# Step tables read from the joined kernels, which are written block by block; small loads issued after a product

## The chip, the cores and the metric

One core of a Trainium2 chip. TensorE (PE; PEld is its weight load) multiplies, VectorE (DVE), ScalarE (ACT) and GpSimd (POOL) work element by element, SyncE (SP) and GpSimd issue DMAs. Each engine runs its own list of instructions in a fixed order. The metric is the device time of one execution in microseconds; the median of 3 runs is 1490.93 us (1490.72 to 1493.30).

## What is computed

Two blocks of two layers each on 256 tokens of 1024 features, all in float32. The first block: an even mixer, a banded attention, each followed by attention over a memory and by a squared-ReLU MLP. The second block, cut to what matters here:

```python
mix = diff_attention(u, w_qkv, q_gain, k_gain, lam_vecs, ...)   # layer 0: rotary tables times gains
h = h + mix; h = h + squared_relu_mlp_2(rms_norm(h), w_up, w_down)
mix = s5_layer(u, a_re, a_im, log_dt, b_re, b_im, c_re, c_im, d_skip, w_glu)   # layer 1
# per group of 16 features, 64 complex states, forward and backward:
states = associative_scan(a_bar, u @ b_bar);  y = (states @ c).real
y = y_forward + y_backward + d_skip * u;  val, gate = gelu(y) @ w_glu;  out = val * sigmoid(gate)
```

## The kernel before

Matrix products are made of three products of split operands: each weight is loaded into `raw`, ScalarE makes its rounded part `whi` (L47, L53), VectorE the rest `wlo` (L49, L58). `raw` has 4 buffers, `whi` and `wlo` 10 each; SyncE issues all weight loads in order, and waits there for a free buffer.

The state-space layer works in steps of 8 tokens. For each of 64 groups it needs tables that depend on parameters alone: `e` (tokens to states), `g` (states to tokens) and `t`, the step table, that takes 8 tokens directly to 8 tokens. They are made by `ssm_tables`, a generator over 16 blocks of 4 groups, and kept in DRAM. Blocks 0 to 7 are made during the last MLP of the first block (`first_block`, L1781), blocks 8 to 15 during the first MLP of the second (`second_block`, L1812). The MLP calls `step(1)` at 49 places (L392, L323, L367), which lets the generator go on by `rate` turns each; `step(1000)` at L397 drains it before the last products. The generator has 35 yields for eight blocks; the second one then runs `ssm_prefetch`, which loads the first tables of the state-space stage. The vector work of the tables is at lower priority (`self.low(90)`).

A block's lag kernels go from `kl` to `d_kl` in DRAM, a row of 144 for each of 4 x 2 x 16 (group, direction, feature). After the last of eight blocks two DMAs join the directions in `d_ks` (rows of 240, forward in 112:240, backward in 0:112; L1450, L1451). Eight DMAs (L1456) then write the table of 8 shifts, each a window of 128 at offset 16 r, to `d_tt`. All these are issued by GpSimd. `load_units` loads 8 groups of `d_tt` in one DMA of 512 KB from SyncE (L1482); there are 8 such units `t`. `load_phases` (L1494) loads the rotation tables `tbs` of the scan, also from SyncE.

`diff`, the attention between those two MLPs, issues six small loads at its start (L644 to L652), then `part(D)`, the products of the keys, then `rotations()` on VectorE (L657 to L674), which needs the loads. Ahead of it in program order stands the end of the MLP: `residual` for each half t of the tokens, with a root on GpSimd (L171), its product with `rsq` (L194), the addition to X (L200) and the transposes `tp` (L140) that the next products need.

The order on each engine is not the program's: a planner places each instruction by priority and by the time at which it reckons its inputs to be ready, and that order is then fixed.

Of the kernel before, what the change touches and what calls it, by code (L numbers as in the profile page):

```python
# [413 lines left out]
class Attn:  # L414
# [224 lines left out]
    def diff(self, pool, w_qkv, gain, q_gain, k_gain, lam_vecs, subln, w_o, cos2, sin2, done):  # L639

        nc = self.nc
        cs = pool.tile([128, 2, 64], F32, tag="cos", name="cos")
        sn = pool.tile([128, 2, 64], F32, tag="sin", name="sin")
        nc.sync.dma_start(out=cs, in_=cos2.rearrange("(t p) e -> p t e", p=128))  # L644
        nc.sync.dma_start(out=sn, in_=sin2.rearrange("(t p) e -> p t e", p=128))
        gq, gk = (pool.tile([128, 64], F32, tag="g" + nm, name="qkg") for nm in "qk")
        nc.sync.dma_start(out=gq, in_=q_gain.partition_broadcast(128))
        nc.sync.dma_start(out=gk, in_=k_gain.partition_broadcast(128))
        sg = pool.tile([128, KT], F32, tag="sg", name="sg")
        nc.sync.dma_start(out=sg, in_=subln)  # L650
        lv = pool.tile([128, 4, 64], F32, tag="lv", name="lv")
        nc.sync.dma_start(out=lv, in_=lam_vecs.partition_broadcast(128))  # L652
        nlam = pool.tile([128, 1], F32, tag="nlam", name="nlam")
        tabs = {}

        def rotations():
            for nm, g in (("k", gk), ("q", gq)):  # L657
                ta = pool.tile([128, 2, 64], F32, tag="ta" + nm, name="ta")
                tb = pool.tile([128, 2, 64], F32, tag="tb" + nm, name="tb")
                if nm == "q":  # L660
                    nc.vector.tensor_scalar(out=g, in0=g, scalar1=0.125, scalar2=None, op0=ALU.mult)
                for t in range(2):
                    nc.vector.tensor_tensor(out=ta[:, t, :], in0=cs[:, t, :], in1=g, op=ALU.mult)
                    nc.vector.tensor_tensor(out=tb[:, t, 0:32], in0=sn[:, t, 0:32], in1=g[:, 32:64], op=ALU.mult)
                    nc.vector.tensor_tensor(out=tb[:, t, 32:64], in0=sn[:, t, 32:64], in1=g[:, 0:32], op=ALU.mult)
                tabs[nm] = (ta, tb)
# [477 lines left out]
class Ssm:  # L1144
# [3 lines left out]
    def ssm_scratch(self, dram):  # L1148
# [6 lines left out]
        self.d_ks = dram.tile([NG, 16, 240], F32, name="d_ks")  # L1155
        self.d_tt = dram.tile([128, NG, 128], F32, name="d_tt")

# [212 lines left out]
    def ssm_tables(self, blocks, bc4, gain, d_rows, dmask):  # L1370
# [6 lines left out]
        with self.tc.tile_pool(name="tab", bufs=1, reuse_waits="tile") as pool:  # L1377
# [33 lines left out]
            def second(k, bc, bm, er, gr):  # L1411
                cr, ci = bc[:, :, 2], bc[:, :, 3]
                for g2 in range(2):
# [6 lines left out]
                    nc.gpsimd.dma_start(out=self.d_e[k, :, g2 * 512:g2 * 512 + 512], in_=eo.rearrange("p g r n -> p (g r n)"))  # L1420
                    yield
                ps = self.ps.tile([128, 144], F32, tag="ps", name="klag")
                for j in range(4):
# [10 lines left out]
                nc.gpsimd.dma_start(out=self.d_kl[k], in_=kl)  # L1434

            last = None
            for k in list(blocks) + [None]:
# [8 lines left out]
                yield  # L1446
            a0, a1 = blocks[0], blocks[-1] + 1
            kl5 = self.d_kl.rearrange("a (q d i) n -> a q d i n", q=4, d=2)
            ks = self.d_ks.rearrange("(a q) i n -> a q i n", q=4)
            nc.gpsimd.dma_start(out=ks[a0:a1, :, :, 112:240], in_=kl5[a0:a1, :, 0, :, 0:128])  # L1450
            nc.gpsimd.dma_start(out=ks[a0:a1, :, :, 0:112], in_=kl5[a0:a1, :, 1, :, 32:144])  # L1451
            yield
            n = 4 * (a1 - a0)
            for r in range(8):
                src = bass.AP(self.d_ks.tensor, self.d_ks.offset + 4 * a0 * 16 * 240 + r * 16, [[240, 16], [3840, n], [1, 128]])
                nc.gpsimd.dma_start(out=self.d_tt[r * 16:r * 16 + 16, 4 * a0:4 * a1, :], in_=src)  # L1456
            yield

    def ssm_prefetch(self):
# [9 lines left out]
        for q in range(4):  # L1469
            t = pool.tile([128, 1024], F32, name=f"e{q}")  # L1470
            self.load_units(t, "e", q)
        for q in range(2):
            self.load_units(pool.tile([128, 1024], F32, tag=f"w{q}", name=f"t{q}"), "t", q)

    def load_units(self, tile, kind, i, n=1):

        t = tile.rearrange("p (a n) -> p a n", n=1024)
        if kind == "t":
            src = self.d_tt[:, 8 * i:8 * (i + n), :].rearrange("p (a g) n -> p a (g n)", g=8)
        else:  # L1480
            src = (self.d_e if kind == "e" else self.d_g)[i:i + n].rearrange("a p n -> p a n")
        self.nc.sync.dma_start(out=t, in_=src)  # L1482
        for a in range(n):
# [7 lines left out]
    def load_phases(self, b):  # L1491

        t = self.pre.tile([128, 3, 16, 32], F32, tag="tbs", name="tbs", bufs=2)
        self.nc.sync.dma_start(out=t, in_=self.d_c[b].rearrange("p (a g c) -> p a g c", a=3, g=16))  # L1494
        self.tbs[b] = t
# [241 lines left out]
def first_block(c, A):  # L1737
    tc, nc = c.tc, c.nc
    for l in range(2):
# [38 lines left out]
        with tc.tile_pool(name=f"ff{l}", bufs=1, reuse_waits="tile") as pool:  # L1778
            if l == 1:
                c.later.append(lambda: reorder(c))  # L1780
            c.mlp(pool, A["w_ff1"][l], gc[2], A["w_ff2"][l], lambda t, a, q: c.residual(t, a, post, q), perm=l == 1,  # L1781
                  fill=tables(c, A, range(8)) if l == 1 else c.ssm_scalars(A["ssm_a_re_2"], A["ssm_a_im_2"], A["ssm_log_dt_2"], c.sgn),
                  rate=0.7 if l == 1 else 0.2)

# [14 lines left out]
def tables(c, A, blocks, last=False):  # L1799
    yield from c.ssm_tables(blocks, A["ssm_bc"], A["ssm_g"], c.d_rows, c.dmask)  # L1800
    if last:
        c.ssm_prefetch()


def second_block(c, A, out):
# [5 lines left out]
    with tc.tile_pool(name="ffb0", bufs=1, reuse_waits="tile") as pool:  # L1811
        c.mlp(pool, A["ffn_w_up_2"][0], c.gcols[:, 8, :], A["ffn_w_down_2"][0], lambda t, a, q: c.residual(t, a, None, q, feat=False),  # L1812
              fill=tables(c, A, range(8, 16), last=True), rate=0.85)
    with tc.tile_pool(name="ssm", bufs=1, reuse_waits="tile") as pool:
# [84 lines left out]
```

## Time and profile before

| | us |
|---|---|
| median of 3 runs | 1490.93 |
| profiled execution | 1488.93 |
| its span | 1487.2 |
| TensorE busy | 1414.7 |
| VectorE busy | 1103.8 |
| ScalarE busy | 859.4 |
| GpSimd busy (its DMA issues not counted) | 234.4 |

Times in rows are counted from the start of the span. A number after `[` is idle time of the engine before the instruction, and `<-` names what ended it. `SPq` is SyncE's DMA queue. Busy times of matrix products overlap, since they are pipelined.

### The profile page before, as it was taken

What the parts mean: (1) busy time and instruction counts of PE and PEld (TensorE: products, weight loads), DVE (VectorE), ACT (ScalarE), POOL (GpSimd) and SP (SyncE); (2) the same over time, 40 slices, a digit from 0 to 9 for tenths busy, and PEclk for the clock granted to TensorE, in tenths of its full rate; (3) what the DMA queues carried; (4) which work ended last, traced back from release to release, by engine and by line L of the source; (5) the groups of instructions that cost most, each with busy time, mean ns of one, the idle gap of its engine ahead of it and who ended that gap; (6) DMA issues with size and microseconds to landing.
All of it is one profiled execution on the core that took longest, in us unless ns stands there. A gap on an engine that the chain in (4) does not pass through costs nothing.

```text
span 1487.2 us, 25549 instructions
## 1 busy us (share of the span) xinstructions
PE 1414.7 (95%) x9668; PEld 1231.5 (83%) x9668; DVE 1103.8 (74%) x1965; ACT 859.4 (58%) x1480; POOL 234.4 (16%) x290
## 2 busy tenths in 40 slices
PE   8899999999999999999999789999999878999997
PEld 8897888998889798878888667888889666889895
DVE  7996658997676866569998589889995487665651
ACT  7475547565564665566656557667656463554540
POOL 1232001000010000014634210033551200000000
PEclk9999999999999999999999999999999998999999
DMA  8465535475875356366677734357779977455640
GB/s 302 143 198 170 185 125 177 157 257 193 287 256 184 119 180 200 112 207 207 220 242 265 254 124 142 100 161 241 238 236 334 346 280 262 153 187 180 210 159 29
DMA packets 121236, 298.26 MB, mean 201 GB/s; under 512 B 15129, under 2 KB 24121, under 8 KB 120473
## 3 DMA queue, kind: packets, MB, share of 16 engines
q1 hardware_dynamic: 113848, 271.40, 55.3%
q0 software_dynamic: 7264, 25.24, 4.6%
q8 instruction: 76, 1.25, 0.3%
q14 instruction: 48, 0.39, 0.1%
HBM read 270.15 MB, written 31.62 MB: 203 GB/s over the span
## 4 chain that ended last, share of the span: by engine, by line
PE 73%; DVE 13%; DMA 6%; issue 4%; ACT 3%; POOL 1%; SPq 0%; DVEq 0%; ACTq 0%; POOLq 0%
PE ffacc L217 7%; PE ffacc L219 7%; PE ffacc L218 7%; PE ffps L224 5%; PE ffps L226 5%; PE ffps L225 5%; PE pacc L219 4%; PE pacc L218 4%; PE pacc L217 4%; DVE wlo L58 3%; PE pb L225 3%; PE pb L224 3%; PE pb L226 3%; DMA raw<-in_w_ff 2%; PE ffps L219 2%
## 5 line engine op out<-in xcount | busy, mean ns | idle before, releaser
L58 DVE SCALAR_TENSOR_TENSOR wlo<-raw,gcols,whi 128x512 fp32r<-128x512 f32 (+1 forms) x456 | 356.7, 826 | 75.6 <-ACT whi L53 75.3
L53 ACT ACTIVATE whi<-raw,gcols 128x512 fp32r<-128x512 f32 (+1 forms) x456 | 317.0, 745 | 104.4 <-PE pb L226 17.3
L47 ACT ACTIVATE whi<-raw 128x1024 fp32r<-128x1024 f32 x176 | 182.8, 1055 | 155.6 <-DMA raw<-in_w_ff 59.3
L49 DVE TENSOR_TENSOR wlo<-raw,whi 128x1024 fp32r<-128x1024 f32 x172 | 210.1, 1241 | 84.1 <-ACT whi L47 80.1
L224 PE MATMUL ffps<-hh,whi 128*128 128x256 f32 x768 | 220.2, 287 | 2.7 <-ACT eo L1419 1.5
L226 PE MATMUL ffps<-hl,whi 128*128 128x256 f32 x768 | 218.2, 284 | 0.0
L225 PE MATMUL ffps<-hh,wlo 128*128 128x256 f32 x768 | 217.6, 283 | 0.0
L217 PE MATMUL ffacc<-whi,ah 128*128 128x512 f32 x512 | 204.7, 400 | 0.0
L219 PE MATMUL ffacc<-whi,al 128*128 128x512 f32 x512 | 202.2, 395 | 0.0
L218 PE MATMUL ffacc<-wlo,ah 128*128 128x512 f32 x512 | 202.1, 395 | 0.0
L224 PEld LDWEIGHTS ffps<-hh,whi 128*128 128x128 f32 x768 | 146.0, 190 | 5.3 <-ACT eo L1419 2.0
L225 PEld LDWEIGHTS ffps<-hh,wlo 128*128 128x128 f32 x768 | 145.7, 190 | 0.6
L226 PEld LDWEIGHTS ffps<-hl,whi 128*128 128x128 f32 x768 | 145.8, 190 | 0.0
L219 PEld LDWEIGHTS ffacc<-whi,al 128*128 128x128 f32 x512 | 96.4, 188 | 22.7
L217 PEld LDWEIGHTS ffacc<-whi,ah 128*128 128x128 f32 x512 | 96.5, 188 | 22.5 <-issue 1.8
L218 PEld LDWEIGHTS ffacc<-wlo,ah 128*128 128x128 f32 x512 | 96.5, 189 | 20.8
L225 PE MATMUL pb<-hh,wlo 128*128 128x256 f32 x352 | 101.2, 289 | 2.6 <-DVE wlo L58 2.6
L224 PE MATMUL pb<-hh,whi 128*128 128x256 f32 x352 | 101.2, 290 | 2.2 <-ACT whi L53 2.2
L226 PE MATMUL pb<-hl,whi 128*128 128x256 f32 x352 | 100.8, 287 | 0.0
L171 POOL TENSOR_TENSOR r<-r,mhalf 128x1 f32<-128x1 f32 x32 | 23.3, 730 | 463.9 <-DVE r L170 457.4
L303 ACT ACTIVATE relu<-ffps 128x512 f32<-128x512 f32 x64 | 43.8, 685 | 54.9 <-PE ffps L226 36.4
L225 PEld LDWEIGHTS pb<-hh,wlo 128*128 128x128 f32 x352 | 68.4, 195 | 3.4 <-DVE wlo L58 3.3
(488 smaller groups left out, 3024.9 us busy)
## 6 DMA issues: line engine op xcount, KB each, us to landing
raw<-in_w_ff SPq DMA_DIRECT2D x128, 512.0 KB, 4.6
raw<-in_ffn_w_up SPq DMA_DIRECT2D x64, 512.0 KB, 4.7
raw<-in_ffn_w_down SPq DMA_DIRECT2D x64, 512.0 KB, 4.6
raw<-in_w_mem_kv SPq DMA_DIRECT2D x32, 512.0 KB, 4.7
raw<-in_w_qkv SPq DMA_DIRECT2D x24, 512.0 KB, 4.7
raw<-in_attn_w_qkv SPq DMA_DIRECT2D x24, 512.0 KB, 5.0
raw<-in_w_in_ab SPq DMA_DIRECT2D x20, 512.0 KB, 6.5
raw<-in_w_mem_q SPq DMA_DIRECT2D x16, 512.0 KB, 4.6
```

Source lines behind the costliest of these rows:

```text
L47: nc.scalar.activation(out=hi, in_=src, func=AF.Copy)
L49: eng.tensor_tensor(out=lo, in0=src, in1=hi.bitcast(F32), op=ALU.subtract)
L53: nc.scalar.activation(out=hi[:, a], in_=src[:, a], func=AF.Copy, scale=g)
L58: nc.vector.scalar_tensor_tensor(out=lo[:, a], in0=src[:, a], scalar=g, in1=hi[:, a].bitcast(F32), op0=ALU.mult, op1=ALU.subtract)
L171: nc.gpsimd.tensor_tensor(out=r, in0=r, in1=self.mhalf[:, 0:1], op=ALU.pow)
L217: nc.tensor.matmul(o, xh, wh[:, s], start=first, stop=False)
L218: nc.tensor.matmul(o, xh, wl[:, s], start=False, stop=False)
L219: nc.tensor.matmul(o, xl, wh[:, s], start=False, stop=last)
L224: nc.tensor.matmul(out, wh, xh, start=first, stop=False)
L225: nc.tensor.matmul(out, wl, xh, start=False, stop=False)
L226: nc.tensor.matmul(out, wh, xl, start=False, stop=last)
L303: nc.scalar.activation(out=o, in_=ps if view is None else ps.rearrange("p (f c j) -> p f c j", f=2, j=8), func=AF.Relu)
```

## The change

The second re-layout and `d_tt` go; a unit `t` is loaded by eight DMAs of 16 partitions straight from `d_ks`, one for each shift. The two joining DMAs are issued for each block, for block k - 1 during block k (`shifted`), for the last after two more yields. `ssm_prefetch` yields once before its loads of `t`. The six small loads of `diff` move into `rotations()`, after `part(D)`. Phase tables 2 and 3 are loaded from GpSimd's queue. The rates of the two generators go from 0.7 to 0.9 and from 0.85 to 0.95.

```diff
--- before.py
+++ after.py
@@ -641,19 +641,19 @@
         nc = self.nc
         cs = pool.tile([128, 2, 64], F32, tag="cos", name="cos")
         sn = pool.tile([128, 2, 64], F32, tag="sin", name="sin")
-        nc.sync.dma_start(out=cs, in_=cos2.rearrange("(t p) e -> p t e", p=128))
-        nc.sync.dma_start(out=sn, in_=sin2.rearrange("(t p) e -> p t e", p=128))
         gq, gk = (pool.tile([128, 64], F32, tag="g" + nm, name="qkg") for nm in "qk")
-        nc.sync.dma_start(out=gq, in_=q_gain.partition_broadcast(128))
-        nc.sync.dma_start(out=gk, in_=k_gain.partition_broadcast(128))
         sg = pool.tile([128, KT], F32, tag="sg", name="sg")
-        nc.sync.dma_start(out=sg, in_=subln)
         lv = pool.tile([128, 4, 64], F32, tag="lv", name="lv")
-        nc.sync.dma_start(out=lv, in_=lam_vecs.partition_broadcast(128))
         nlam = pool.tile([128, 1], F32, tag="nlam", name="nlam")
         tabs = {}
 
         def rotations():
+            nc.sync.dma_start(out=cs, in_=cos2.rearrange("(t p) e -> p t e", p=128))
+            nc.sync.dma_start(out=sn, in_=sin2.rearrange("(t p) e -> p t e", p=128))
+            nc.sync.dma_start(out=gq, in_=q_gain.partition_broadcast(128))
+            nc.sync.dma_start(out=gk, in_=k_gain.partition_broadcast(128))
+            nc.sync.dma_start(out=sg, in_=subln)
+            nc.sync.dma_start(out=lv, in_=lam_vecs.partition_broadcast(128))
             for nm, g in (("k", gk), ("q", gq)):
                 ta = pool.tile([128, 2, 64], F32, tag="ta" + nm, name="ta")
                 tb = pool.tile([128, 2, 64], F32, tag="tb" + nm, name="tb")
@@ -1153,7 +1153,6 @@
         self.d_rho = dram.tile([128, NG], F32, name="d_rho")
         self.d_kl = dram.tile([16, 128, 144], F32, name="d_kl")
         self.d_ks = dram.tile([NG, 16, 240], F32, name="d_ks")
-        self.d_tt = dram.tile([128, NG, 128], F32, name="d_tt")
 
     def cmul(self, pool, outr, outi, xr, xi, yr, yi, neg_i=False, tag="ct", second=None):
 
@@ -1419,6 +1418,8 @@
                     A.activation(out=eo.rearrange("p g r n -> p (g r) n"), in_=ps, func=AF.Copy)
                     nc.gpsimd.dma_start(out=self.d_e[k, :, g2 * 512:g2 * 512 + 512], in_=eo.rearrange("p g r n -> p (g r n)"))
                     yield
+                    if g2 == 0 and k > blocks[0]:
+                        shifted(k - 1)
                 ps = self.ps.tile([128, 144], F32, tag="ps", name="klag")
                 for j in range(4):
                     o = ps[j * 32:j * 32 + 32]
@@ -1433,6 +1434,14 @@
                 V.scalar_tensor_tensor(out=kl[:, 0:16], in0=dmask, scalar=d_rows[:, k:k + 1], in1=kl[:, 0:16], op0=MU, op1=AD)
                 nc.gpsimd.dma_start(out=self.d_kl[k], in_=kl)
 
+            kl5 = self.d_kl.rearrange("a (q d i) n -> a q d i n", q=4, d=2)
+            ks = self.d_ks.rearrange("(a q) i n -> a q i n", q=4)
+
+            def shifted(k):
+
+                nc.gpsimd.dma_start(out=ks[k, :, :, 112:240], in_=kl5[k, :, 0, :, 0:128])
+                nc.gpsimd.dma_start(out=ks[k, :, :, 0:112], in_=kl5[k, :, 1, :, 32:144])
+
             last = None
             for k in list(blocks) + [None]:
                 if k is not None:
@@ -1444,16 +1453,9 @@
                     yield from second(*last)
                 last = cur
                 yield
-            a0, a1 = blocks[0], blocks[-1] + 1
-            kl5 = self.d_kl.rearrange("a (q d i) n -> a q d i n", q=4, d=2)
-            ks = self.d_ks.rearrange("(a q) i n -> a q i n", q=4)
-            nc.gpsimd.dma_start(out=ks[a0:a1, :, :, 112:240], in_=kl5[a0:a1, :, 0, :, 0:128])
-            nc.gpsimd.dma_start(out=ks[a0:a1, :, :, 0:112], in_=kl5[a0:a1, :, 1, :, 32:144])
-            yield
-            n = 4 * (a1 - a0)
-            for r in range(8):
-                src = bass.AP(self.d_ks.tensor, self.d_ks.offset + 4 * a0 * 16 * 240 + r * 16, [[240, 16], [3840, n], [1, 128]])
-                nc.gpsimd.dma_start(out=self.d_tt[r * 16:r * 16 + 16, 4 * a0:4 * a1, :], in_=src)
+            for _ in range(2):
+                yield
+            shifted(blocks[-1])
             yield
 
     def ssm_prefetch(self):
@@ -1469,6 +1471,7 @@
         for q in range(4):
             t = pool.tile([128, 1024], F32, name=f"e{q}")
             self.load_units(t, "e", q)
+        yield
         for q in range(2):
             self.load_units(pool.tile([128, 1024], F32, tag=f"w{q}", name=f"t{q}"), "t", q)
 
@@ -1476,10 +1479,12 @@
 
         t = tile.rearrange("p (a n) -> p a n", n=1024)
         if kind == "t":
-            src = self.d_tt[:, 8 * i:8 * (i + n), :].rearrange("p (a g) n -> p a (g n)", g=8)
+            for r in range(8):
+                src = bass.AP(self.d_ks.tensor, self.d_ks.offset + 8 * i * 16 * 240 + r * 16, [[240, 16], [3840, 8 * n], [1, 128]])
+                self.nc.sync.dma_start(out=tile[r * 16:r * 16 + 16].rearrange("p (g n) -> p g n", n=128), in_=src)
         else:
             src = (self.d_e if kind == "e" else self.d_g)[i:i + n].rearrange("a p n -> p a n")
-        self.nc.sync.dma_start(out=t, in_=src)
+            self.nc.sync.dma_start(out=t, in_=src)
         for a in range(n):
             self.unit[kind, i + a] = t[:, a]
 
@@ -1491,7 +1496,8 @@
     def load_phases(self, b):
 
         t = self.pre.tile([128, 3, 16, 32], F32, tag="tbs", name="tbs", bufs=2)
-        self.nc.sync.dma_start(out=t, in_=self.d_c[b].rearrange("p (a g c) -> p a g c", a=3, g=16))
+        q = self.nc.gpsimd if b > 1 else self.nc.sync
+        q.dma_start(out=t, in_=self.d_c[b].rearrange("p (a g c) -> p a g c", a=3, g=16))
         self.tbs[b] = t
 
     def ssm(self, pool, X, w_glu):
@@ -1780,7 +1786,7 @@
                 c.later.append(lambda: reorder(c))
             c.mlp(pool, A["w_ff1"][l], gc[2], A["w_ff2"][l], lambda t, a, q: c.residual(t, a, post, q), perm=l == 1,
                   fill=tables(c, A, range(8)) if l == 1 else c.ssm_scalars(A["ssm_a_re_2"], A["ssm_a_im_2"], A["ssm_log_dt_2"], c.sgn),
-                  rate=0.7 if l == 1 else 0.2)
+                  rate=0.9 if l == 1 else 0.2)
 
 
 def reorder(c):
@@ -1799,7 +1805,7 @@
 def tables(c, A, blocks, last=False):
     yield from c.ssm_tables(blocks, A["ssm_bc"], A["ssm_g"], c.d_rows, c.dmask)
     if last:
-        c.ssm_prefetch()
+        yield from c.ssm_prefetch()
 
 
 def second_block(c, A, out):
@@ -1810,7 +1816,7 @@
                A["attn_w_o_2"], A["cos"], A["sin"], lambda t, a: c.residual(t, a))
     with tc.tile_pool(name="ffb0", bufs=1, reuse_waits="tile") as pool:
         c.mlp(pool, A["ffn_w_up_2"][0], c.gcols[:, 8, :], A["ffn_w_down_2"][0], lambda t, a, q: c.residual(t, a, None, q, feat=False),
-              fill=tables(c, A, range(8, 16), last=True), rate=0.85)
+              fill=tables(c, A, range(8, 16), last=True), rate=0.95)
     with tc.tile_pool(name="ssm", bufs=1, reuse_waits="tile") as pool:
         c.ssm(pool, X, A["ssm_w_glu_2"])
     c.pre_pool.__exit__(None, None, None)
```

## Rows read from the trace of the kernel before

**Rows 1.** Page, part 1: busy us, share of the span, instructions, by engine.
```profile
PE 1414.7 (95%) x9668; PEld 1231.5 (83%) x9668; DVE 1103.8 (74%) x1965; ACT 859.4 (58%) x1480; POOL 234.4 (16%) x290
```

**Rows 2.** Waits of TensorE, whole span: waiting, for whom, total us, times, longest.
```profile
PE tp L140 <- issue: 11.1, 1, 11.1
...
PE utp L1538 <- DVE xp L1522: 9.2, 1, 9.2
...
PE yp L1617 <- DMA g<-d_g: 4.0, 3, 2.1
...
PE yp L1607 <- DMA t<-d_tt: 0.2, 1, 0.2
```

**Rows 3.** Timeline, 836 to 862 us: start, us, engine, line, operation [idle before].
```profile
839.38 0.77 POOL L171 TENSOR_TENSOR r<-r,mhalf 128x1 f32<-128x1 f32 x1
...
846.94 5.43 DVE L58 SCALAR_TENSOR_TENSOR wlo<-raw,gcols,whi 128x512 fp32r<-128x512 f32 x8 [3.03 <-ACT whi L53]
...
848.80 0.46 SPq L644 DMA_DIRECT2D cos<-in_cos  x1
...
851.80 1.77 SPq L42 DMA_DIRECT2D raw<-in_attn_w_qkv  x3
...
853.23 0.20 DVE L661 TENSOR_SCALAR qkg<-qkg 128x64 f32<-128x64 f32 x1 [0.87 <-DMA qkg<-in_attn_q_gain]
...
856.17 0.29 DVE L669 TENSOR_TENSOR lp<-lv 128x128 f32<-128x128 f32 x1 [1.18 <-DMA lv<-in_attn_lambda]
...
857.32 0.15 DVE L194 TENSOR_TENSOR r<-r,rsq 128x1 f32<-128x1 f32 x1
857.51 1.41 DVE L200 SCALAR_TENSOR_TENSOR X<-y,r,X 128x512 f32<-128x512 f32 x2
...
858.36 1.94 PE L140 MATMUL tp<-ident,X 128*128 128x128 f32 x8 [11.09 <-issue]
```

**Rows 4.** Timeline of GpSimd, 834 to 840 us.
```profile
834.22 5.09 POOL L1456 DMA_DIRECT2D d_tt<-d_ks  x8 [2.19 <-DMA d_ks<-d_kl]
```

**Rows 5.** Stretches: length, busy us by engine (instructions), TensorE clock, DMA share, GB/s.
```profile
655.00:800.00 145.00, 137.02 (x1023) 121.01 (x1022) 130.45 (x199) 93.11 (x161) 66.70 (x68) 0.99 0.66 218
...
880.00:920.00 40.00, 35.94 (x186) 27.98 (x186) 39.28 (x103) 25.91 (x56) 2.40 (x1) 1.00 0.37 119
...
990.00:1140.00 150.00, 150.00 (x1159) 132.04 (x1158) 139.31 (x216) 94.14 (x170) 70.78 (x77) 1.00 0.71 239
...
1193.00:1260.00 67.00, 54.91 (x1013) 43.02 (x1012) 52.88 (x65) 36.23 (x55) 0.00 (x0) 0.90 0.74 262
```

**Rows 6.** Timeline of TensorE, 858 to 870 us, after the gap.
```profile
860.23 0.79 PE L217 MATMUL acc<-whi,hh 128*128 128x512 f32 x1
...
862.62 0.39 PE L217 MATMUL acc<-whi,hh 128*128 128x512 f32 x1
...
865.42 1.04 PE L140 MATMUL tp<-ident,X 128*128 128x128 f32 x8
```

**Rows 7.** Timeline of SyncE's queue, 1080 to 1300 us.
```profile
1213.91 0.79 SPq L1482 DMA_DIRECT2D t<-d_tt  x2
...
1225.26 1.35 SPq L1482 DMA_DIRECT2D t<-d_tt  x2
```

**Rows 8.** Timeline of TensorE, 1200 to 1300 us.
```profile
1221.28 0.64 PE L1607 MATMUL yp<-t,ut 128*32 128x128 f32 x16 [0.16 <-DMA t<-d_tt]
...
1230.19 0.66 PE L1617 MATMUL yp<-g,h 128*32 128x128 f32 x8 [2.14 <-DMA g<-d_g]
```

**Rows 9.** DMA, 833 to 850 us: packets, MB, share; issues, KB, us to landing.
```profile
q0 software_dynamic: 749, 2.38, 45.2%
...
q1 hardware_dynamic: 1114, 2.15, 38.6%
...
d_tt<-d_ks POOLq DMA_DIRECT2D x8, 256.0 KB, 4.6
```

**Rows 10.** DMA, whole span: issues, KB each, median us to landing.
```profile
d_kl<-kl POOLq DMA_DIRECT2D x16, 72.0 KB, 3.6
```

## The prediction

> **What bounds the kernel now.** I read four views, in this order. First the busy times: TensorE is busy 1414.7 of 1487.2 us [rows 1], so only 72.5 us can be won without taking products away, and the change takes none away. Then the waits of TensorE, to see where those 72.5 us lie [rows 2]: the longest single one, 11.1 us, stands before a transpose `tp` with no releaser named ("issue"); the next, 9.2 us, stands before the state-space stage; that stage's waits for DMA are small (4.0 and 0.2 us). Third, the timeline around the 11.1 us wait, on all engines [rows 3]. Here the reader sees the cause. The reciprocal root for token half 0 is done on GpSimd at 839.38 + 0.77 = 840.15 us, but VectorE multiplies by it (L194) only at 857.32. VectorE takes its instructions in one fixed order, and in front of L194 stand eight weight splits (846.94 to 852.37) and then the rotation tables of the attention (L661 to L674, 853.23 to 857.40). These wait twice for the small loads (0.87 and 1.18 us), which SyncE issued only at 848.80. X is ready after 857.5, and TensorE, done with its last product at 858.36 - 11.09 = 847.27, starts the transposes at 858.36. Why does L194 stand so late? Just before it the GpSimd queue held the eight writes of the second re-layout, 5.09 us of issue behind a wait of 2.19 us for the joined kernels [rows 4]. The planner that fixed the order must have reckoned with a late root; that is inferred. Last, the stretches [rows 5]: in both MLPs with table work VectorE is nearly full (130.45 of 145 us, 139.31 of 150), in the attention it is full (39.28 of 40), and in the state-space stage TensorE works 54.91 of 67 us.
>
> **The change part by part**, against the profiled execution: 1488.93 us, which is its span of 1487.2 and 1.73 around it. The median of the runs shown, 1490.93, lies 2.00 higher; I make the sum on 1488.93 and add the 2.00 at the end.
>
> *The second re-layout goes (16 DMAs of 0.63 us on GpSimd).* 16 x 0.63 = 10.1 us of GpSimd time, no part of it under TensorE's path except the place just named: with rate 0.7 the 49 steps of the first MLP give 34.3 turns of a generator that has 35 yields, so shift and re-layout fell into the drain right before the last products, ahead of the root. With rate 0.9 the 36 yields are through at step 40, nine steps earlier, and nothing stands ahead of the root. In the second MLP the turns end at step 39 instead of 43; TensorE has no wait there, so I count nothing.
>
> *The six small loads go behind the products of the keys.* Their issues, 848.80 to 851.80 or 0.50 us each, are only moved [rows 3]; three weight loads that stood behind them (1.77 us) come 3.0 us sooner. The table instructions on VectorE (853.23 to 857.40, with the two waits) can no longer be planned ahead of the loads, and so fall behind L194.
>
> *What both are worth together.* Upper end: X is ready at 840.15 + 0.19 + 1.41 = 841.8, before TensorE needs it, and all 11.09 us go. The clock adds something: after the gap eight transposes take 1.94 us against 1.04 seven us later, and a product 0.79 us against 0.39 [rows 6]; 0.90 for the transposes and about 0.8 for the next products make 1.7 us, so 12.8. Lower end: the tables stay ahead of L194 and their loads come later by four weight issues of 0.6 us, a loss of 2.4. Between them: only the tables go behind, L194 stays behind the eight splits; then 857.32 - 852.4 = 4.9 us. What is late next: VectorE. From 880 to 920 us it idles 0.72 us and TensorE already waits 4.06 us there [rows 5]; products that come 11 us early meet tables, splits and softmax that don't. VectorE itself idled 3.03 + 0.87 + 1.18 = 5.1 us in [rows 3], which the earlier X lets it use; the rest of a lead can only come from a better order of its work. I take 12.8 less 4 = **-8.8 us**, nearer to the upper end, because both things ahead of L194 are removed.
>
> *Shifted writes block by block.* 32 GpSimd issues of about 0.65 us in place of 4: 28 x 0.65 = 18.2 us more, less the 10.1 above; GpSimd works 66.70 of 145 us in the first MLP [rows 5], so they are hidden. Each now waits for its block's joined kernel, queued three yields ahead (over three steps; 49 steps fill some 150 us, so 3 us each), while that lands in 3.6 us [rows 10]. If the wait did last, products on GpSimd that feed the tables would stand behind it. **0**; ends 0 and +2 (half the 3.6 us in one block in four).
>
> *Higher rates.* The same table work wants 0.7/0.9 of the time in the first MLP and 0.85/0.95 in the second. VectorE has 14.55 and 10.69 us to spare there [rows 5], so it becomes oversubscribed for a while and the tables fall behind schedule, which costs nothing unless TensorE waits at a transpose of a table. TensorE idles 7.98 us in 655 to 800 and nothing in 990 to 1140. Ends: -2 (a quarter of that idle time goes) and +8 (it doubles); I take **+1**.
>
> *Step tables from the joined kernels: eight DMAs of 64 KB for one of 512 KB, on eight tables.* A table now costs SyncE 0.79/2 = 0.40 us [rows 7]. Eight pieces by 0.46 us (the `cos` issue, [rows 3]) are 3.7 us; by GpSimd's 0.63 they would be 5.0. A pair so takes 7.4 us of SyncE instead of 0.79, **6.6 us** more, four pairs in all. The first is loaded in the MLP's tail (TensorE waits for nothing), the second is issued before the stage begins. The third is issued at 1213.91 and its second half is already awaited for 0.16 us at 1221.28 [rows 7, 8]; its last piece would be issued at 1213.91 + 7.4 = 1221.3 instead of 1214.7. TensorE stands in order, so the second half of block 1's outputs waits with it. Half of that is taken up by the wait for `g` that follows anyway (2.14 us at 1230.19, [rows 8]). The fourth is issued at 1225.26 [rows 7]; before its use, as before the first two pairs, TensorE had no wait for `t` at all [rows 2]. Ends: 0 (planner sorts the products of `t` back) and three pairs on the path, 3 x 6.6 = +19.8. I take **+2**: one pair, the one with a row that shows no slack, cut by the `g` wait.
>
> In bytes the pieces cost the same: in 833 to 850 us the re-layout, reading 512 B at a time in 16 rows, moved 2.38 MB at 45.2% of 16 engines, the weights 2.15 MB at 38.6% [rows 9], 5.3 against 5.6 MB per unit of share. And pieces issued back to back overlap: eight of 256 KB leave within 5.09 us [rows 4] and each lands 4.6 us after its issue [rows 9].
>
> The Trainium skill ("DMA: Bandwidth & Descriptors", Anatomy of one DMA) speaks against this part: a DMA costs about 2.0 us fixed plus its bytes at 436 GB/s, and its rules for kernel authors say that transfers under 64 KB are mostly overhead. Worked out from that page, as an estimate, eight pieces paid one after the other would be 17.2 us against 3.2, and three such pairs +84 us. The overlap in the rows of the re-layout does not bear that out: by it the fixed part is latency and is paid once. The same mechanism at the price of the rows is rival C.
>
> *Two phase loads from GpSimd's queue.* GpSimd has nothing to do from 1193 to 1260 [rows 5]; the loads wait for the same VectorE products as before and leave SyncE free. **0**; ends -1 and +1 (the issues, 0.46 against 0.63, and a landing like its neighbours').
>
> Sum: -8.8 + 0 + 1 + 2 + 0 = -5.8, so 1483.1 on the profiled execution and **1485.1 us** on the median.
>
> **The rivals.**
> *A. VectorE gives the lead back.* For it: the attention's 39.28 of 40 us. Against: 5.1 us of idle time are there to be used, and after 946 us VectorE is less full. Then only those 5.1 us stay: -5.1 + 3 = -2.1, 1488.8.
> *B. The change does not do what it says at the root:* the planner still puts L194 behind splits or tables. For it: nothing fixes their order in the text of the kernel, and the order was planned badly once. Against: the tables now hang on later loads. Then 0 to -1, plus 3: 1493.
> *C. Slower: the step tables arrive late in the state-space stage.* One mechanism: SyncE issues in order, and 16 pieces take 7.4 us. It decides when two of the three late pairs are on the path in full: 2 x 6.6 = 13.2, less 8.8, plus 1: 1496.3; from 1.2 pairs (8.8 - 1 = 7.8 us) on it makes the kernel slower. For it: the 0.16 us wait without slack. Against: of all waits for `t` only one shows, 0.2 us in total [rows 2].
> *D. Better than forecast:* the attention keeps all 12.8 us, and the planner orders the step tables without a wait: -12.8, 1478.
>
> **How the numbers follow.** Forecast 0.48 (own range 1481 to 1489), A 0.17, B 0.11, C 0.14, D 0.10. From no change one can tell 0.2%, 3.0 us, so faster is below 1487.9. Faster: 0.44 of the forecast's, 0.07 of A, 0.10 of D = 0.61. Same: 0.04 + 0.10 + 0.06 (of B) = 0.20. Slower: 0.05 of B and 0.14 of C = 0.19. The range reaches to D's 1477 and to C's 1496.
>
> **What would show it.** Right: the wait of 11 us before `tp` is gone, L194 follows the root within 2 us, the clock does not fall there, the tables come after L200, and TensorE's waits in the attention grow by some 4 us. In the state-space stage eight issues per table on SyncE, some 0.46 us each, and a wait of 2 to 4 us before `yp<-t` of block 2. Wrong: L194 still behind eight splits (B), a step of more than 5 us before `yp<-t` (C), or waits at transposes of tables in the MLPs, which would make the rates the main term.

## The result, and the profile after

The changed kernel takes 1529.75 us (median of 4 runs, 1523.87 to 1532.19), the kernel before 1490.83 beside it: ratio 1.0251, 95% interval 1.0233 to 1.0269. It is 38.9 us slower, and far outside the forecast range of 1477 to 1496. The profiled execution took 1531.52 us, its span is 1529.7; TensorE is busy 1434.0 us in as many products, 9668, as before [rows 1].

To find where the 42.5 us between the two profiled spans went, cut both spans at instructions that each kernel has: first `ffacc` of the first block, its last `ffacc` (end of the MLP that makes the first tables), first `ffacc` of the second block, first `utp` (start of the state-space stage), last `gp`, end. Starts of these instructions, subtracted, in us:

| stretch | before | after | difference |
|---|---|---|---|
| to the first `ffacc` | 268.7 | 267.9 | -0.8 |
| first block, first to last `ffacc`; tables 0 to 7 | 578.2 | 598.2 | +20.0 |
| root and attention | 175.9 | 164.7 | -11.2 |
| second block's first MLP, tables 8 to 15 | 170.1 | 185.4 | +15.3 |
| state-space stage | 101.1 | 120.0 | +18.9 |
| rest | 193.2 | 193.5 | +0.3 |

The attention gained what was forecast and a little more. The two MLPs and the state-space stage, for which the forecast had 0, +1 and +2, lost 54 us.

Waits of TensorE after, as in [rows 2] (whole span):

```profile
engine line waited for: us in total, times, longest us
PE etp L1417 <- DVE er L1168: 15.9, 4, 7.4
...
PE yp L1623 <- DVE h L1617: 7.2, 1, 7.2
PE val L217 <- ACT hh L1649: 6.6, 1, 6.6
PE klag L1427 <- issue: 4.8, 2, 2.9
```

The 11.1 us before `tp` are gone: VectorE now waits for the root and multiplies at once (timeline), before the last product of the MLP,

```profile
856.94 0.16 DVE L194 TENSOR_TENSOR r<-r,rsq 128x1 f32<-128x1 f32 x1 [0.68 <-POOL r L171]
857.13 1.41 DVE L200 SCALAR_TENSOR_TENSOR X<-y,r,X 128x512 f32<-128x512 f32 x2
```

In their place stand waits at `etp`, the transposes of the tables being made, two in the first MLP (6.6 us) and two in the second (9.3 us), and in the first also waits at `klag`, the products of the lag kernels. The longest one, on TensorE:

```profile
1107.90 1.41 PE L1417 MATMUL etp<-ident,er 128*128 128x128 f32 x4 [7.43 <-DVE er L1168]
```

and VectorE in front of it (timeline):

```profile
1102.20 2.97 DVE L1167 TENSOR_TENSOR gr<-pk,bc 128x512 f32<-128x512 f32 x1
1105.09 2.06 DVE L58 SCALAR_TENSOR_TENSOR wlo<-raw,gcols,whi 128x512 fp32r<-128x512 f32 x3
1107.08 0.68 DVE L1168 TENSOR_TENSOR er<-er,cmt 128x512 f32<-128x512 f32 x1
```

TensorE stands at `etp` while VectorE, in its own fixed order, still makes another table (`gr`) and three weight splits. Each of the four waits at `etp` is paid twice: behind each of them the clock stood at 1.2 GHz for some us (behind the longest, from 1107.9 to 1112, the granted clock was 0.50). Stretches of after (length, busy us of each engine, mean granted clock as a share of 2.4 GHz, DMA; a mean below 1 means that part of the stretch ran at 1.2 GHz):

```profile
core 0: us, PE busy (x) PEld busy (x) DVE busy (x) ACT busy (x) POOL busy (x), PEclk, DMA share, GB/s
655.00:863.00 208.00, 189.61 (x1320) 166.76 (x1319) 154.14 (x235) 121.71 (x205) 81.61 (x96) 0.94 0.61 201
...
1100.00:1120.00 20.00, 12.51 (x110) 11.70 (x110) 15.94 (x24) 8.48 (x18) 11.28 (x16) 0.74 0.59 197
...
1216.00:1260.00 44.00, 30.49 (x644) 26.05 (x644) 32.23 (x46) 20.28 (x35) 1.21 (x2) 0.81 0.86 275
1260.00:1280.00 20.00, 13.30 (x46) 10.23 (x46) 6.10 (x7) 3.60 (x6) 0.00 (x0) 0.74 0.48 114
1280.00:1336.00 56.00, 50.57 (x470) 41.57 (x470) 33.98 (x42) 28.15 (x41) 0.57 (x1) 0.91 0.68 223
```

and the same work before, beside [rows 5]:

```profile
655.00:847.00 192.00, 183.56 (x1326) 160.25 (x1324) 157.69 (x234) 119.25 (x201) 79.15 (x89) 0.99 0.70 234
...
1193.00:1294.00 101.00, 88.00 (x1160) 70.03 (x1160) 71.31 (x92) 52.45 (x82) 0.55 (x1) 0.93 0.66 226
```

In the first MLP TensorE idles 208 - 189.61 = 18.4 us instead of 8.4, and is busy 6.05 us longer with nearly the same products (1320 and 1326 in the rows), at a clock of 0.94 instead of 0.99. These 16 us are most of the 20.0 of that stretch. In the second MLP, between 1100 and 1120, around the long wait, the clock is 0.74. In the state-space stage the same sum (120 - 94.4 = 25.6 us idle instead of 13.0, busy 6.4 us longer) gives the 18.9. VectorE's busy time in the first MLP did not grow (154.14 of 208 us against 157.69 of 192): over the whole of it VectorE did not lack time. It was late at single places, with tables that TensorE was already waiting for.

In the stage, SyncE's step tables (timeline; consecutive issues of one kind in one row, from the first start to the last end):

```profile
1163.90 15.80 SPq L1484 DMA_DIRECT2D t<-d_ks  x16
...
1163.90 12.02 SPq L1484 DMA_DIRECT2D t<-d_ks  x8
...
1239.17 13.46 SPq L1484 DMA_DIRECT2D t<-d_ks  x16
1252.73 2.58 SPq L1487 DMA_DIRECT2D g<-d_g  x4
1259.28 16.76 SPq L1484 DMA_DIRECT2D t<-d_ks  x16
```

A pair of tables takes 13.5 to 16.8 us of SyncE, not 7.4, and `g` waits behind it. Of the first pair, the first eight pieces take 12.0 us, the second eight 3.8. The reason is in the landing times. A load `e` issued at 1161.34 lands 10.4 us later, the next, of 1162.11, after 11.8 us, so at 1171.7 and 1173.9 (DMA issues in these moments: count, KB each, us to landing):

```profile
e<-d_e SPq DMA_DIRECT2D x1, 512.0 KB, 10.4
...
e<-d_e SPq DMA_DIRECT2D x1, 512.0 KB, 11.8
```

and the eighth DMA after each is issued just then (timeline):

```profile
1171.73 0.30 SPq L1484 DMA_DIRECT2D t<-d_ks  x1
...
1173.97 0.30 SPq L1484 DMA_DIRECT2D t<-d_ks  x1
```

In this program SyncE's DMAs take turns through eight semaphores, and an issue waits until the DMA eight before it has landed: the trace shows it in all 156 cases where it has that landing. Eight loads of 512 KB on the way are 4 MB; eight pieces are 0.5 MB.

Not all of the time is of this kind. In the last three pairs (waits of SyncE, 1216 to 1300)

```profile
SPq L1484 <- DMA e<-d_e: 13.8, 9, 2.4
...
SPq L1484 <- PE val L218: 7.6, 1, 7.6
```

and the 7.6 us, a wait for TensorE and not for a landing, stand in the pair of 16.76 us.

TensorE itself does not wait for `t` in this stage. Its two longest waits there are 7.2 us at a product of `g`, for `h`, and 6.6 us at `val`, both in the list above. The first runs back to VectorE, which waited for a phase table `tbs` that GpSimd had issued at 1235.89 and that landed 8.6 us later (timelines of VectorE and TensorE):

```profile
1244.51 0.69 DVE L1583 TENSOR_TENSOR ra<-z,tbs 128x512 f32<-128x512 f32 x1 [3.30 <-DMA tbs<-d_c]
...
1250.03 3.38 PE L1623 MATMUL yp<-g,h 128*32 128x128 f32 x64 [7.23 <-DVE h L1617]
```

So it is not `t` itself that comes too late in this kernel, but other loads. Which of them makes up how much of the 18.9 us was not separated.

### The profile page after: what moved, and what is told of

Its sections match the earlier page's. It is cut to its first block, busy times and chain, and to the rows that moved or that the text cites. A ratio compares the mean times of both kernels' runs of the same rounds, so it can differ in the third digit from the quotient of the medians.

```text
span 1529.7 us, 25606 instructions
## 1 busy us (share of the span) xinstructions
PE 1434.0 (94%) x9668; PEld 1249.2 (82%) x9668; DVE 1100.9 (72%) x1965; ACT 861.8 (56%) x1480; POOL 233.3 (15%) x304
## 4 chain that ended last, share of the span: by engine, by line
PE 63%; DVE 14%; DMA 9%; issue 6%; ACT 4%; POOL 3%; SPq 0%; DVEq 0%; ACTq 0%; POOLq 0%
PE ffacc L219 6%; PE ffacc L217 6%; PE ffacc L218 6%; PE ffps L226 5%; PE ffps L224 5%; PE ffps L225 4%; DVE wlo L58 3%; PE pacc L218 3%; PE pacc L219 3%; PE pacc L217 3%; PE pb L224 2%; PE pb L225 2%; PE pb L226 2%; DMA raw<-in_w_ff 2%; PE ffps L219 1%
## 5 line engine op out<-in xcount | busy, mean ns | idle before, releaser
L224 PE MATMUL ffps<-hh,whi 128*128 128x256 f32 x768 | 225.6, 294 | 2.8 <-ACT kl L1433 2.8
L226 PE MATMUL ffps<-hl,whi 128*128 128x256 f32 x768 | 222.7, 290 | 0.0
L225 PE MATMUL ffps<-hh,wlo 128*128 128x256 f32 x768 | 222.1, 289 | 0.0
L224 PEld LDWEIGHTS ffps<-hh,whi 128*128 128x128 f32 x768 | 151.3, 197 | 5.1 <-ACT kl L1433 3.1
L225 PEld LDWEIGHTS ffps<-hh,wlo 128*128 128x128 f32 x768 | 151.1, 197 | 0.6
L226 PEld LDWEIGHTS ffps<-hl,whi 128*128 128x128 f32 x768 | 150.6, 196 | 0.0
L171 POOL TENSOR_TENSOR r<-r,mhalf 128x1 f32<-128x1 f32 x32 | 27.0, 845 | 496.4 <-DVE r L170 490.0
```

The source lines that it names most:

```text
L171: nc.gpsimd.tensor_tensor(out=r, in0=r, in1=self.mhalf[:, 0:1], op=ALU.pow)
L224: nc.tensor.matmul(out, wh, xh, start=first, stop=False)
L225: nc.tensor.matmul(out, wl, xh, start=False, stop=False)
L226: nc.tensor.matmul(out, wh, xl, start=False, stop=last)
```

## The experiments

Their stretches, as in the table above (us, one profiled execution each). Labels with `a_` are the changed kernel with something undone, those with `b_` and `k_` the kernel before with something added. FB is the first block from its first to its last `ffacc`, AT root and attention, M2 the second block's first MLP, SS the state-space stage:

| kernel | median | FB | AT | M2 | SS |
|---|---|---|---|---|---|
| a_old_rates | 1505.41 | 585.0 | 163.1 | 170.7 | 120.3 |
| b_new_rates | 1513.95 | 600.3 | 174.8 | 174.5 | 100.4 |
| b_small_loads | 1492.59 | 579.4 | 175.9 | 169.7 | 101.4 |
| b_all_sp | 1491.46 | 578.6 | 176.2 | 173.6 | 99.3 |
| a_ph_sync_old_rates | 1515.50 | 584.2 | 164.8 | 171.9 | 128.6 |
| a_tt_sp_old_rates | 1501.44 | 584.1 | 177.9 | 170.4 | 104.8 |
| a_t_pool_old_rates | 1512.05 | 584.9 | 165.3 | 170.8 | 125.4 |
| k_lam | 1493.36 | 581.3 | 176.0 | 172.0 | 98.8 |
| a_tt8_old_rates | 1521.05 | 584.7 | 175.9 | 171.8 | 120.1 |
| k_defer3 | 1484.66 | 580.9 | 168.8 | 170.1 | 100.8 |
| b_blocks | 1495.51 | 584.7 | 173.5 | 173.0 | 98.1 |
| k_defer3_ph | 1485.24 | 581.5 | 169.0 | 169.7 | 103.7 |

**The rates.** Undone in the changed kernel (`a_old_rates`; the diff shows this one), done alone in the one before (`b_new_rates`):

```diff
-                  rate=0.9 if l == 1 else 0.2)
+                  rate=0.7 if l == 1 else 0.2)
...
-              fill=tables(c, A, range(8, 16), last=True), rate=0.95)
+              fill=tables(c, A, range(8, 16), last=True), rate=0.85)
```

> The changed kernel with the two rates of before (0.7 and 0.85); all else changed. Theory 1 (the rates): the first MLP takes 15.7 us and the second 15.3 us longer in the changed kernel because tables are due before VectorE and GpSimd can make them and TensorE waits in order at their transposes; with the old rates both go back, 1529.75 - 31 = about 1499. Theory 2 (block-by-block writes on GpSimd, which wait for each block's joined kernel and hold up the products that feed the tables): the MLPs stay as they are, about 1528. The state-space stage stays 19 us longer than before under both.

> The kernel before with the two new rates alone (0.9 and 0.95). Theory 1 (the rates): 1490.8 + 31 = about 1522, with waits of TensorE before table transposes. Theory 2 (block-by-block writes): 1491, no change. The 11 us wait before the attention's first transposes stays under both, since the joining writes and the re-layout still end on GpSimd.

Undone: 1505.41, ratio to before 1.0084 [1.0064, 1.0104], so 1529.75 - 1505.41 = 24 us come back; in the profiled executions it is 13.2 in FB and 14.7 in M2. Alone: 1513.95 against 1492.46, 1.0132 [1.0107, 1.0157], +22.1 in FB and 4.4 in M2. The rates are the main term, 22 to 24 us, though not the 31 that both expectations had. In M2 they cost 15 us only together with the rest of the change; what in the rest does that was not separated.

With the rates alone TensorE waits at other places of the same work: in the first MLP not for `er`, but at `klag` and behind ScalarE's copy `eo` of the transposes (waits of TensorE, 655 to 872):

```profile
PE klag L1426 <- issue: 5.8, 3, 3.5
PE ffps L224 <- ACT eo L1419: 4.5, 2, 3.4
```

The clock there is 0.94, as in the changed kernel.

**The small loads alone** (`b_small_loads`, moved as in the change):

> The kernel before with the six small loads moved behind the key products, and nothing else. The prediction's step: the tables fall behind L194, worth 4.9 us at least, 1486. Rival: the planner put the loads behind eleven weight loads before and does so now, and the tables stay ahead of L194: 1491, with the 11 us wait unchanged.

1492.59 against 1492.46, ratio 1.0000 [0.9987, 1.0013]. The move does nothing by itself: the planner issues the loads at the same place in SyncE's order, after the first five and before the next three of the attention's weights.

**The writes at the end of the tables issued by SyncE** (`b_all_sp`), in the kernel before:

```diff
-            nc.gpsimd.dma_start(out=ks[a0:a1, :, :, 112:240], in_=kl5[a0:a1, :, 0, :, 0:128])
+            nc.sync.dma_start(out=ks[a0:a1, :, :, 112:240], in_=kl5[a0:a1, :, 0, :, 0:128])
...
-                nc.gpsimd.dma_start(out=self.d_tt[r * 16:r * 16 + 16, 4 * a0:4 * a1, :], in_=src)
+                nc.sync.dma_start(out=self.d_tt[r * 16:r * 16 + 16, 4 * a0:4 * a1, :], in_=src)
```

> The kernel before, with the two joining writes and the eight re-layout writes issued by SyncE instead of GpSimd, and nothing else. Theory: these ten DMAs ahead of the root on GpSimd made the planner place L194 late; without them on that queue the 11 us wait goes, as it did in the changed kernel (9.7 us there): 1481. Rival: the wait went through another part of the change: 1491, or above it by what SyncE's waits for the joined kernels hold up in weight loads (some 5 us per MLP).

1491.46, ratio 0.9994 [0.998, 1.0008]: no gain. The first product of the attention starts at 846.7 instead of 860.2 us, 13.5 earlier, but the whole stretch is as long as before (176.2 us, before 175.9). 13 us later 8.4 us are lost at once (waits of TensorE, 846 to 1030; then ScalarE's timeline):

```profile
PE acc L217 <- ACT whi L53: 8.4, 1, 8.4
```

```profile
869.25 0.20 ACT L672 ACTIVATE ls<-ls 128x2 f32<-128x2 f32 x1 [8.84 <-DVE ls L671]
869.36 3.16 ACT L53 ACTIVATE whi<-raw,gcols 128x512 fp32r<-128x512 f32 x5
```

Five weight splits stand behind a small exponential, which waits for VectorE's tables.

**That exponential moved behind the first queries** (`k_lam`; in the diff `lam`, the lambda scalars, as a function of its own; the writes stay on SyncE as in the last diff):

```diff
+        def lam():
             lp = pool.tile([128, 2, 64], F32, tag="lp", name="lp")
...
         q0 = prep(0, a, "q", put_q[0])
+        lam()
```

> The kernel before with joining and re-layout issued by SyncE (alone 1491.5 us: the 11.1 us wait ahead of the attention is gone, but 13 us later TensorE waits 8.4 us for whi), and the lambda scalars of the attention (product, sum, exponential, difference) moved behind the preparation of the first queries. Theory L1 (ScalarE's order: the five splits whi stand behind the exponential ls at 869.25, which waits for VectorE's L671, which stands behind the keys' norm): the wait of 8.4 us goes, and with it the low clock after it (0.66 in 860 to 880): 1479 to 1484. Theory L2 (VectorE is full in the attention and gives the lead back wherever it stands): another wait takes its place, 1488 to 1492.

1493.36, ratio 1.0012 [1.0001, 1.0023]. The wait changes its name (waits of TensorE, whole span):

```profile
PE acc L218 <- DVE wlo L58: 9.3, 1, 9.3
```

L1 falls. L2's number holds, but not quite its reason: VectorE idles 6.4 us a little ahead of it, waiting for the keys' squares, with the splits queued behind them. There it is the planner's order that gives the lead back, not a lack of VectorE time.

**The state-space stage.** Four versions of the changed kernel with the old rates: phase loads back on SyncE (`a_ph_sync_old_rates`); step tables through the second layout, written by SyncE, in one DMA each (`a_tt_sp_old_rates`); the pieces issued by GpSimd, phase loads on SyncE (`a_t_pool_old_rates`); and the second layout read in eight DMAs of 16 partitions, with rows of 4 KB (`a_tt8_old_rates`). Each diff shows the line that tells it from the others.

```diff
-        q = self.nc.gpsimd if b > 1 else self.nc.sync
-        q.dma_start(out=t, in_=self.d_c[b].rearrange("p (a g c) -> p a g c", a=3, g=16))
+        self.nc.sync.dma_start(out=t, in_=self.d_c[b].rearrange("p (a g c) -> p a g c", a=3, g=16))
```

> The changed kernel with the rates of before (0.7 and 0.85) and all phase loads on SyncE again; against the one with the old rates alone (1505.4 us, state-space stage from the first utp to the last gp 120.4 us, before 101.1). Theory S1 (eight DMAs on the way): in the trace of the changed kernel a piece of a step table is issued only when the DMA issued eight before it on SyncE's queue has landed (e issued at 1161.34 lands 10.37 us later, the eighth one after it is issued at 1171.73), so the 64 pieces hold up SyncE whatever the phase loads do: stage 116 to 121, total 1501 to 1507. Theory S4 (the phase loads on GpSimd's queue come late, DVE waited 3.3 us for one that took 8.6 us): stage down by 3.3 us and more, total 1490 to 1500.

```diff
+            src = self.d_tt[:, 8 * i:8 * (i + n), :].rearrange("p (a g) n -> p a (g n)", g=8)
...
+        self.nc.sync.dma_start(out=t, in_=src)
```

> The changed kernel with the old rates, the second re-layout back (issued by SyncE) and each step table read from it in one DMA of 512 KB; blockwise writes, small loads and phase loads stay as changed. Theory S1 (64 pieces on SyncE): the stage falls from 120.4 to 101 to 104 us, total 1486 to 1492, if the first MLP keeps the 8 us that the version with old rates lost there. Theory S4 (phase loads): stage stays at 115 or more, total 1500 or more. If the blockwise writes cost the 8 us of the first MLP, it still ends some 6 to 8 us later than before (846.9).

```diff
-                self.nc.sync.dma_start(out=tile[r * 16:r * 16 + 16].rearrange("p (g n) -> p g n", n=128), in_=src)
+                self.nc.gpsimd.dma_start(out=tile[r * 16:r * 16 + 16].rearrange("p (g n) -> p g n", n=128), in_=src)
```

> The changed kernel with the old rates, phase loads on SyncE, and the 64 pieces of the step tables issued by GpSimd, which has next to nothing else to do in the stage. S1 (the pieces hold up SyncE's other loads, and these the pieces): stage 101 to 108 us, total 1486 to 1493. S3 (the 512-byte packets themselves are slow on the DMA engines): stage 115 to 120, total 1500 to 1506.

```diff
+            for r in range(0, 128, 16):
+                self.nc.sync.dma_start(out=t[r:r + 16], in_=src[r:r + 16])
```

> As the version that reads each step table from the second layout (1501.4 us; stage from the first utp to the last gp 104.7 us, against 120.4 with 64 pieces read from the joined kernels), but each table in eight DMAs of 16 partitions with 4 KB rows instead of one. It has the count of DMAs of the change and not its 512-byte rows. Theory N (the number of DMAs: eight on the way per queue, each waits for the landing of the eighth before it): stage 115 to 121, total 1512 to 1518. Theory P (the 512-byte rows): stage 104 to 108, total 1500 to 1505.

Phase loads back: the stage grows from 120.3 to 128.6 us (total 1515.50, 1.0154 [1.0129, 1.018]). That is outside both expectations; S4 falls, and beside the pieces the move to GpSimd had gained 8 us. Here TensorE does wait for `t`, 6.3 us in two waits. One DMA per table: 104.8, just above S1's 101 to 104; the total, 1501.44, misses its 1486 to 1492, for the attention's lead is lost (AT 177.9 against 163.1), as in the kernel with the writes on SyncE above. Eight DMAs of the same bytes in 4 KB rows: 120.1, as with 512-byte rows, so N holds and P falls. Its total, 1521.05, lies above the 1512 to 1518 expected; its profiled execution has a span of 1514.6. Both versions with eight DMAs write 16 partitions with each, so that shape was not told apart from the number. Waits of SyncE for the pieces in that kernel, 1190 to 1310, show the same thing as in the changed one, 17.2 us behind earlier landings:

```profile
SPq L1490 <- DMA e<-d_e: 8.8, 7, 1.8
SPq L1490 <- DMA g<-d_g: 8.4, 5, 2.3
```

Pieces on GpSimd: 125.4, only 3.2 less than with all on SyncE, where S1 had 101 to 108 and S3 115 to 120. Freeing SyncE isn't enough: on GpSimd 24 pieces took a median of 7.3 us to land (1219 to 1242), and they wait there for TensorE and for one another (waits of GpSimd, 1180 to 1320). What sets the 125.4 was not followed further.

```profile
POOL t L1484 <- PE yp L1612: 19.7, 1, 19.7
POOL t L1484 <- DMA t<-d_ks: 11.6, 12, 2.6
```

**The shifted writes block by block** (`b_blocks`), alone in the kernel before (`shifted` as in the change, re-layout kept):

> The kernel before with the shifted writes issued block by block on GpSimd (32 instead of 4) and all else as before, the second re-layout too. Theory B1 (the writes hold up GpSimd's products for the tables: the version with the old rates lost 6.8 us in the first MLP): first MLP (first to last ffacc, 578.2 us before) 583 to 586, total 1495 to 1499. Theory B0 (that loss came from elsewhere): first MLP 577 to 580, total 1489 to 1493.

FB 584.7 as B1 said, total 1495.51, ratio 1.0042 [1.0028, 1.0057]: 6.5 us lost in FB, of which AT and SS give some back. The longest wait there, 5.7 us, ends with ScalarE's `eo`, which stands in its order behind a split whose weights landed late. How the writes bring that about, by GpSimd's products as B1 has it or otherwise, was not shown.

**The writes moved behind the MLP** (`k_defer3`), unchanged and on GpSimd, emitted with the second block's tables:

```diff
+            def join():
                 nc.gpsimd.dma_start(out=ks[a0:a1, :, :, 112:240], in_=kl5[a0:a1, :, 0, :, 0:128])
...
+            if a0 == 0:
+                self.join = join
+            else:
+                join()
...
 def tables(c, A, blocks, last=False):
+    if last:
+        c.join()
```

> The kernel before with its joining and re-layout writes unchanged, on GpSimd, but emitted with the tables of the second MLP instead of at the end of the first; in the order as built the reciprocal root then has two or three of the ten writes ahead of it instead of all ten, and the weight splits stay ahead of the attention's products. Theory R (the lead at the root was lost by those writes; it is kept where the splits stay ahead): the 11.1 us wait shrinks to 0 to 4 us and the attention keeps it: 1480 to 1486. Rival (the lead is given back as in the two kernels with the writes on SyncE): 1489 to 1493.

1484.66 us, ratio 0.9963 [0.9945, 0.9981]: faster than both kernels. One write is issued ahead of the root (at 830.62), the other nine behind it, and VectorE multiplies by the root 1.0 us after it is done (timelines of GpSimd and VectorE):

```profile
839.40 0.56 POOL L171 TENSOR_TENSOR r<-r,mhalf 128x1 f32<-128x1 f32 x1 [8.12 <-DVE r L170]
839.92 0.68 POOL L1453 DMA_DIRECT2D d_ks<-d_kl  x1
...
839.64 1.41 DVE L58 SCALAR_TENSOR_TENSOR wlo<-raw,gcols,whi 128x512 fp32r<-128x512 f32 x2 [0.40 <-ACT whi L53]
840.97 0.15 DVE L194 TENSOR_TENSOR r<-r,rsq 128x1 f32<-128x1 f32 x1
841.04 0.75 DVE L58 SCALAR_TENSOR_TENSOR wlo<-raw,gcols,whi 128x512 fp32r<-128x512 f32 x1
841.71 1.41 DVE L200 SCALAR_TENSOR_TENSOR X<-y,r,X 128x512 f32<-128x512 f32 x2
```

The splits stay between these steps, ahead of the attention's products, and most of the lead is kept: AT 168.8, 7.1 less than before, with 4.1 of the 11.1 us of wait left. FB is 2.7 longer.

**The phase loads on GpSimd, added to that** (`k_defer3_ph`):

> The version with the join moved behind the first MLP (1484.7 us, stage 100.8) and, of the change, the two phase loads on GpSimd's queue alone. With the 64 pieces this move gave back 8.2 us of the stage (128.6 to 120.4). Theory F (SyncE's queue was full of pieces; with one DMA per table the move has nothing to free, and its load lands late on a queue of its own): stage 100 to 105, total 1484 to 1489. Theory G (SyncE standing 7.2 us at the phase load, waiting for VectorE, holds up the loads behind it in any kernel): stage 93 to 98, total 1477 to 1482.

1485.24, ratio 0.9957 [0.9937, 0.9977], stage 103.7: F. With one DMA per table the move brings nothing that can be told from noise.

## Why the prediction was wrong, step by step

*Second re-layout and small loads, -8.8.* The size was nearly right (-11.2 in the stretch, the wait of [rows 3] gone), and the signs came: L194 follows the root at once, the tables come after L200. What the prediction only inferred, that the planner put L194 late because of the writes ahead of the root [rows 4], two experiments bear out: with the writes on SyncE, or nine of the ten behind the root, VectorE multiplies early. The small loads alone change nothing (ratio 1.0000); whether their move helps to keep the lead once the writes are gone was not run. Rival A, VectorE giving the lead back, did not happen here. It does happen where the same writes stand on SyncE, but by the order of ScalarE and VectorE rather than by their being full.

*Higher rates, +1, with an end at +8.* This step failed most: 22 to 24 us. I wrote that tables behind schedule cost nothing unless TensorE waits at a transpose of a table, named such waits as the sign that the rates would be the main term, and then bounded them by doubling the idle time of [rows 5]. TensorE waits at four (15.9 us), the idle time of the whole first MLP more than doubled, and behind each of the four waits the clock was low for the next products, which the bound left out though [rows 6] had the price. A warning was there: with VectorE at 130.45 of 145 us and TensorE's work in one fixed order with the tables', asking for the tables earlier moves TensorE's instructions ahead of what they wait for, unless VectorE is earlier too. In the second MLP, "no wait there" before was read as room; it was the state that the rate, with the rest of the change, then ended.

*Step tables in pieces, +2.* Rival C had the right engine and the right order, that pieces hold up SyncE, but the price too low and the path only in part: its sign, a step of more than 5 us before `yp<-t`, did not come in the changed kernel, where other loads are late. 0.46 us per piece is what an issue takes where nothing is in the way (eight in 3.8 us). But eight DMAs may be on the way at once, so a piece behind loads of 512 or 768 KB waits for one of them to land, up to 2.5 us: 13.5 to 16.0 us for each of the first three pairs. The rows that gave 0.46 were six small loads [rows 3]. The worth of the pieces is 120.3 - 104.8 = 15.5 us of the stage. In the Trainium skill ("DMA: Bandwidth & Descriptors", Anatomy of one DMA, a section on DMAs that GpSimd issues), the 2 us of a DMA are mostly the wait for its completion. The trace agrees as far as it goes for SyncE's pieces: some 0.43 us of issue, and 2.4 us at least from issue to landing, the moving of the bytes included. The estimate of +84 us that I worked out from that page by adding them up is refuted by the eight pieces that leave in 3.8 us. But completion does count, once eight are on the way; I dismissed it as latency that is paid once.

*Shifted writes, 0 (0 to +2).* 6.5 us in the first MLP when done alone, 4.3 in the total. I had called them hidden because GpSimd works only 66.70 of 145 us; a busy share does not show that. With the new rates it is not additive: the whole change costs 20.0 there, the rates alone 22.1.

*Phase loads, 0.* Right where a table is one DMA (1485.24 against 1484.66); beside the pieces they gained 8 us.

So a sum of -5.8 became +38.9 in the medians (+42.5 in the profiled spans), mostly through two terms, the rates and the pieces, that were sized from rows of an uncrowded moment. The 0.14 given to rival C and the 8 us end of the rates were too little, and above all the two were never allowed to come together.

## What to carry to other kernels

Where instructions of a filler (tables for later) stand in the same in-order engine as the products, a higher rate paid nothing here, since the engines that make the tables were not earlier too: look for the first wait at a filler instruction, and add the clock that the wait costs. Before a load is cut into pieces, count how many DMAs its queue has on the way, and price a piece by the landing of the one that it must wait for, not by its issue. A lead won ahead of a stage is kept only if what the stage needs next (here the weight splits) is not ordered behind something late.

## What was not expected of the hardware

Eight DMAs of 64 KB leave SyncE in 3.8 us when nothing is ahead of them, and in 12.0 us behind loads of 512 and 768 KB; the rows' length (512 B or 4 KB) made no difference to the stage (120.3 and 120.1 us), and one DMA in place of eight did (104.8). A VectorE instruction of 0.68 us took 2.97 us in one place (L1167, above) while GpSimd was working on tables; the cause was not looked into.
